# Batched matmul: four DRAM rows per partition, all transfers on one queue, casts and evacuations exchanged

## The chip, the core and the metric

The kernel runs on one core of one Trainium2 chip. The metric is the device time of one execution in microseconds; of the kernel before there are three runs, with a median of 133.25 us (132.75 to 133.29).

## The reference

For each of 16 batches the kernel computes the product of the transposed `a` with `b`. Both inputs are 512 x 512 float32, `a` is laid out as (k, m) and `b` as (k, n), and the output is float32 as well:

```python
batch, m, k, n = 16, 512, 512, 512
np.matmul(a.transpose(0, 2, 1), b).astype(np.float32)
```

`a` and `b` of one batch are 1 MB each, and so is the output: 33.55 MB are read and 16.78 MB are written in all.

## The kernel before

The unit of work is a batch. For each batch the kernel loads a whole matrix `a` and a whole matrix `b` into SBUF, casts both to bfloat16, multiplies them in 16 matmuls, and stores the whole output matrix. The contraction index k is split into KO = 4 groups of 128. The view `a_v` (line 24) is "bat (ko ki) m -> bat ki ko m": partition ki holds the DRAM rows ki, 128 + ki, 256 + ki and 384 + ki. A row is 512 float32, so each partition is filled from four separate pieces of 2 KB that lie 256 KB apart. `b_v` (line 25) is the same for `b`, and `out_v` (line 26) for the output, with the output row index m split into MO = 4 groups in the same way.

Every kind of buffer exists NB = 6 times. `load(bi)` (lines 50 to 53) issues the two 1 MB loads of a batch, one on the queue of SyncE (SP) and one on the queue of GpSimd (POOL), in turns: `a` of an even batch and `b` of an odd one go through SP. `cast(bi)` (lines 55 to 58) lets ScalarE (ACT) cast both matrices, 128 x 2048 elements at a time. `compute(bi)` (lines 60 to 73) makes, for each of the four groups mo of 128 output rows, an accumulation of four matmuls (line 65) into one of eight PSUM banks, and VectorE (DVE) copies the bank to the float32 output tile (line 72). The stationary operand of a matmul is a 128 x 128 block of contiguous columns of the cast `a`; the moving operand is 128 x 512 of the cast `b`. At the end ACT issues the store of the batch (line 73).

The order of the work is that of the Python loop, engine by engine: loads run five batches ahead of the matmuls and casts four batches ahead. ACT therefore has the casts of batch bi + 4 ahead of the store of batch bi in its queue. The transfers of the three queues (SP, POOL and ACT) share the core's 16 DMA engines. A DMA instruction waits on semaphores for the buffer it overwrites, and on that of an earlier DMA where a semaphore is used again.

Of the kernel before, what the change touches and what calls it, by code (L numbers as in the profile page):

```python
# [1 line left out]

# [4 lines left out]


@with_exitstack
def kernel(  # L10
    ctx: ExitStack,
    tc: tile.TileContext,
    a: bass.AP,
    b: bass.AP,
    out: bass.AP,
):
    nc = tc.nc
    P = 128
    batch, K, M = a.shape
    _, _, N = b.shape  # L20
    KO = K // P
    MO = M // P

    a_v = a.rearrange("bat (ko ki) m -> bat ki ko m", ki=P)
    b_v = b.rearrange("bat (ko ki) n -> bat ki ko n", ki=P)
    out_v = out.rearrange("bat (mo mi) n -> bat mi mo n", mi=P)

    f32 = mybir.dt.float32
    bf = mybir.dt.bfloat16
    NB = 6  # L30
    a_pool = ctx.enter_context(tc.tile_pool(name="a_pool", bufs=1))
    b_pool = ctx.enter_context(tc.tile_pool(name="b_pool", bufs=1))
    abf_pool = ctx.enter_context(tc.tile_pool(name="abf_pool", bufs=1))
    bbf_pool = ctx.enter_context(tc.tile_pool(name="bbf_pool", bufs=1))
    o_pool = ctx.enter_context(tc.tile_pool(name="o_pool", bufs=1))
    psum = ctx.enter_context(tc.tile_pool(name="ps", bufs=1, space=bass.MemoryType.PSUM))

    a_ts = [a_pool.tile([P, KO, M], f32, name=f"a{j}") for j in range(NB)]
    b_ts = [b_pool.tile([P, KO, N], f32, name=f"b{j}") for j in range(NB)]
    abf_ts = [abf_pool.tile([P, KO, M], bf, name=f"abf{j}") for j in range(NB)]  # L40
    bbf_ts = [bbf_pool.tile([P, KO, N], bf, name=f"bbf{j}") for j in range(NB)]
    o_ts = [o_pool.tile([P, MO, N], f32, name=f"o{j}") for j in range(NB)]
    psum_ts = [psum.tile([P, N], f32, name=f"ps{j}") for j in range(8)]

    in_eng = [nc.sync, nc.gpsimd]
    out_eng = nc.scalar

    engs = [nc.sync, nc.gpsimd]

    def load(bi):  # L50
        j = bi % NB
        engs[bi % 2].dma_start(a_ts[j][:], a_v[bi])  # L52
        engs[(bi + 1) % 2].dma_start(b_ts[j][:], b_v[bi])  # L53

    def cast(bi):
        j = bi % NB
        nc.scalar.copy(out=abf_ts[j][:], in_=a_ts[j][:])  # L57
        nc.scalar.copy(out=bbf_ts[j][:], in_=b_ts[j][:])  # L58

    def compute(bi):  # L60
        j = bi % NB
        for mo in range(MO):
            pt = psum_ts[(bi * MO + mo) % 8]
            for ko in range(KO):
                nc.tensor.matmul(  # L65
                    pt[:],
                    abf_ts[j][:, ko, mo * P:(mo + 1) * P],
                    bbf_ts[j][:, ko, :],
                    start=(ko == 0),
                    stop=(ko == KO - 1),  # L70
                )
            nc.vector.tensor_copy(out=o_ts[j][:, mo, :], in_=pt[:])  # L72
        nc.scalar.dma_start(out_v[bi], o_ts[j][:])  # L73

    for bi in range(min(NB - 1, batch)):
        load(bi)
    for bi in range(min(NB - 2, batch)):
        cast(bi)
    for bi in range(batch):
        if bi + NB - 1 < batch:  # L80
            load(bi + NB - 1)
        if bi + NB - 2 < batch:
            cast(bi + NB - 2)
        compute(bi)


# [1 line left out]
_INS = ['a', 'b']  # L88
_OUTS = [((16, 512, 512), 'float32')]


# [23 lines left out]
```

## Time and profile before

| What | Value |
|---|---|
| Median of three runs | 133.25 us |
| Profiled execution, span from first to last instruction | 131.4 us |
| Median of the runs less that span | 1.85 us |
| Busy share of the span: PE, DVE, ACT, POOL | 51%, 33%, 46%, 9% |
| DMA in the span | 50.38 MB, mean 383 GB/s |
| The chain that ended last, share on DMA | 73% |
| Mean of one matmul, one weight load, one PSUM copy, one cast | 429, 108, 691, 1896 ns |

The profiled execution's own time is known by its span alone; the 1.85 us between it and the median of the runs are taken as what lies around the span. A busy share tells how long an engine had work, and the 40 slices tell when. The share of a DMA queue in a window is the sum of its packets' durations over 16 engines times the window, so a packet's mean duration can be worked out from the share and the packet count. The shares of all queues can add up to a little over 100%, since a packet begins before the one ahead of it on the engine has ended.

### The profile page before, as it was taken

The numbers are of one execution on the slowest core, as the hardware profiler recorded it, in microseconds if no ns is written. First come the engines' busy times: TensorE is split into PE (matmuls) and PEld (weight loads), VectorE is DVE, ScalarE is ACT, GpSimd is POOL, SyncE is SP. The second block draws the span as 40 slices with busy tenths as digits, with TensorE's granted clock in tenths as the row PEclk, the third lists the DMA queues.
The fourth block names the chain that finished last, engine by engine and source line by source line (L and its number), as shares of the span: only waits on it lengthen the run. The fifth ranks groups of instructions, "written<-read, shape, count | busy, mean of one in ns | idle before, by whom it ended". The sixth has DMA issues, their size and how long they took to land.

```text
span 131.4 us, 806 instructions
## 1 busy us (share of the span) xinstructions
PE 67.5 (51%) x251; PEld 27.6 (21%) x256; DVE 43.9 (33%) x64; ACT 60.4 (46%) x33; POOL 12.3 (9%) x20
## 2 busy tenths in 40 slices
PE   0000899656406975004994049912992894991000
PEld 0000334223102331001341014401340341440000
DVE  0000248462501356000466006720474446672000
ACT  3054396923088140069310696049809949900000
POOL 6700220220003100002200022000000000000000
PEclk9999999999995599955589658997799999999555
DMA  2999999999999999999999999999999999999991
GB/s 88 362 390 390 383 393 386 390 385 384 387 390 402 414 411 406 413 416 406 410 409 416 410 408 413 413 384 393 409 358 403 409 406 403 409 409 409 409 397 64
DMA packets 21252, 50.38 MB, mean 383 GB/s; under 512 B 768, under 2 KB 768, under 8 KB 21248
## 3 DMA queue, kind: packets, MB, share of 16 engines
q1 hardware_dynamic: 8448, 16.78, 34.2%
q10 hardware_dynamic: 8448, 16.78, 33.0%
q0 software_dynamic: 4352, 16.78, 32.6%
q8 instruction: 2, 0.03, 0.1%
q14 instruction: 2, 0.02, 0.0%
HBM read 33.55 MB, written 16.78 MB: 383 GB/s over the span
## 4 chain that ended last, share of the span: by engine, by line
DMA 73%; SPq 7%; PE 5%; ACT 3%; issue 1%; DVE 1%; ACTq 0%
DMA b<-in_b_dram 54%; DMA a<-in_a_dram 19%; PE ps L65 5%; SPq L52 5%; ACT bbf L58 3%; SPq L53 2%; DVE o L72 1%; ACTq L73 0%; ACTq L57 0%; ACT abf L57 0%; ACTq L58 0%
## 5 line engine op out<-in xcount | busy, mean ns | idle before, releaser
L65 PE MATMUL ps<-bbf,abf 128*128 128x512 bf16 x251 | 67.5, 429 | 51.1 <-ACT bbf L58 50.7
L72 DVE COPY o<-ps 128x512 f32<-128x512 f32 x64 | 43.9, 691 | 75.5 <-PE ps L65 60.9
L57 ACT CAST abf<-a 128x2048 bf16<-128x2048 f32 x16 | 30.3, 1896 | 41.7 <-DMA a<-in_a_dram 37.8
L65 PEld LDWEIGHTS <-abf 128*128 128x128 bf16 x256 | 27.6, 108 | 90.5 <-issue 35.8
L58 ACT CAST bbf<-b 128x2048 bf16<-128x2048 f32 x16 | 30.3, 1895 | 12.2 <-DMA b<-in_b_dram 12.1
L53 POOL DMA_DIRECT2D b<-in_b_dram x8 | 6.1, 766 | 60.0 <-ACT bbf L58 59.2
L52 POOL DMA_DIRECT2D a<-in_a_dram x8 | 6.0, 749 | 7.6 <-ACT abf L57 7.6
L57 ACT ACT_TABLE_LOAD x1 | 1.3, 1283 | 0.7 <-PEq L99 0.7
L99 POOL MEMSET const-float32-0.0<- 128x1 f32 x1 | 0.1, 98 | 0.2 <-issue 0.2
L99 POOL MEMSET const-bfloat16-1.0<- 128x1 bf16 x1 | 0.1, 101 | 0.0
L99 POOL MEMSET const-uint8-127<- 128x1 uint8 x1 | 0.1, 99 | 0.0
L99 POOL MEMSET const-float32-1.0<- 128x1 f32 x1 | 0.1, 98 | 0.0
## 6 DMA issues: line engine op xcount, KB each, us to landing
out_dram<-o ACTq DMA_DIRECT2D x16, 1024.0 KB, 11.6
a<-in_a_dram SPq DMA_DIRECT2D x8, 1024.0 KB, 30.3
b<-in_b_dram SPq DMA_DIRECT2D x8, 1024.0 KB, 28.9
b<-in_b_dram POOLq DMA_DIRECT2D x8, 1024.0 KB, 16.5
a<-in_a_dram POOLq DMA_DIRECT2D x8, 1024.0 KB, 19.9
```

Source lines behind the costliest of these rows:

```text
L52: engs[bi % 2].dma_start(a_ts[j][:], a_v[bi])
L53: engs[(bi + 1) % 2].dma_start(b_ts[j][:], b_v[bi])
L57: nc.scalar.copy(out=abf_ts[j][:], in_=a_ts[j][:])
L58: nc.scalar.copy(out=bbf_ts[j][:], in_=b_ts[j][:])
L65: nc.tensor.matmul(pt[:], abf_ts[j][:, ko, mo * P:(mo + 1) * P], bbf_ts[j][:, ko, :], start=(ko == 0), stop=(ko == KO - 1),)
L72: nc.vector.tensor_copy(out=o_ts[j][:, mo, :], in_=pt[:])
L99: nc = _bacc.Bacc("TRN2", target_bir_lowering=False, num_devices=1)
```

## The change

The three DRAM views are written the other way round: `a_v`, `b_v` and `out_v` now give partition p the four consecutive DRAM rows 4p to 4p + 3. For `a` and `b` this is another split of k, the same for both, so that the sum is the same. For the output, group mo now consists of the rows m = 4 mi + mo. The stationary operand has to hold these columns, so it is taken from the cast `a` with a step of four elements (8 bytes) instead of a contiguous block.

All DMAs are issued by SP: loads of `a` and `b`, and stores. Loads run LAG = 4 batches ahead, and the store of batch i is put behind the loads of batch i + 4. There are now five buffers for loads, three for the cast matrices and six for outputs. The casts move from ACT to DVE and stand directly ahead of the matmuls of their own batch; the copies from PSUM move from DVE to ACT. The matmuls, their number and order within a batch are the same.

```diff
-    a_v = a.rearrange("bat (ko ki) m -> bat ki ko m", ki=P)
-    b_v = b.rearrange("bat (ko ki) n -> bat ki ko n", ki=P)
-    out_v = out.rearrange("bat (mo mi) n -> bat mi mo n", mi=P)
-    NB = 6
+    a_v = a.rearrange("bat (ki ko) m -> bat ki ko m", ko=KO)
+    b_v = b.rearrange("bat (ki ko) n -> bat ki ko n", ko=KO)
+    out_v = out.rearrange("bat (mi mo) n -> bat mi mo n", mo=MO)
+    LAG = 4
+    NL = LAG + 1
+    NB = 3
+    NO = LAG + 2
...
-    def load(bi):
-        j = bi % NB
-        engs[bi % 2].dma_start(a_ts[j][:], a_v[bi])
-        engs[(bi + 1) % 2].dma_start(b_ts[j][:], b_v[bi])
+    def load(i):
+        nc.sync.dma_start(a_ts[i % NL][:], a_v[i])
+        nc.sync.dma_start(b_ts[i % NL][:], b_v[i])
+    def store(i):
+        nc.sync.dma_start(out_v[i], o_ts[i % NO][:])
-    def cast(bi):
-        j = bi % NB
-        nc.scalar.copy(out=abf_ts[j][:], in_=a_ts[j][:])
-        nc.scalar.copy(out=bbf_ts[j][:], in_=b_ts[j][:])
...
+        nc.vector.tensor_copy(out=af[:], in_=a_ts[i % NL][:])
+        nc.vector.tensor_copy(out=bff[:], in_=b_ts[i % NL][:])
+        a_m = af[:].rearrange("p ko (mi mo) -> p ko mo mi", mo=MO)
...
-                    abf_ts[j][:, ko, mo * P:(mo + 1) * P],
-                    bbf_ts[j][:, ko, :],
+                    a_m[:, ko, mo, :],
+                    bff[:, ko, :],
...
-            nc.vector.tensor_copy(out=o_ts[j][:, mo, :], in_=pt[:])
-        nc.scalar.dma_start(out_v[bi], o_ts[j][:])
+            nc.scalar.copy(out=o[:, mo, :], in_=pt[:])
-    for bi in range(min(NB - 1, batch)):
-        load(bi)
-    for bi in range(min(NB - 2, batch)):
-        cast(bi)
-    for bi in range(batch):
-        if bi + NB - 1 < batch:
-            load(bi + NB - 1)
-        if bi + NB - 2 < batch:
-            cast(bi + NB - 2)
-        compute(bi)
+    for i in range(min(LAG, batch)):
+        load(i)
+    for i in range(batch):
+        if i + LAG < batch:
+            load(i + LAG)
+        compute(i)
+        store(i)
```

How the DMA queue of SP changes is seen in its order. Before, it holds half of the loads; a number behind a name is a buffer's, and the semaphores that an instruction waits for stand in brackets (DMAHW ones are set by transfers that have landed, Activation and DVE by those engines). These are its first rows:

```order
L52 DMA a_73<-in_a_dram 128x4x512
L53 DMA b_80<-in_b_dram 128x4x512
L52 DMA a_75<-in_a_dram 128x4x512
L53 DMA b_82<-in_b_dram 128x4x512
L52 DMA a_77<-in_a_dram 128x4x512
L53 DMA b_84<-in_b_dram 128x4x512
L52 DMA a_73<-in_a_dram 128x4x512 [waits DMAHW0_49,Activation_49]
L53 DMA b_80<-in_b_dram 128x4x512 [waits DMAHW1_49,Activation_49]
```

After the change, the same queue has every transfer. From the fourth batch's loads on it reads:

```order
L46 DMA a_64<-in_a_dram 128x2048
L47 DMA b_69<-in_b_dram 128x2048
L46 DMA a_65<-in_a_dram 128x2048 [waits DMAHW0_49]
L47 DMA b_70<-in_b_dram 128x2048 [waits DMAHW1_49]
L50 DMA out_dram<-o_77 128x2048 [waits DMAHW2_49,Activation_49]
L46 DMA a_61<-in_a_dram 128x2048 [waits DMAHW3_49,DVE_49]
L47 DMA b_66<-in_b_dram 128x2048 [waits DMAHW4_49,DVE_49]
L50 DMA out_dram<-o_78 128x2048 [waits DMAHW5_49,Activation_49]
```

A transfer is now 128 rows of 2048 elements, where it was 128 x 4 rows of 512. Eight semaphores go round, so that each DMA also waits until the eighth one ahead of it has landed, and the loads behind a store can't be issued before ACT has finished that store's tile. At the end of the queue five stores follow one another:

```order
L46 DMA a_61<-in_a_dram 128x2048 [waits DMAHW1_49,DVE_49]
L47 DMA b_66<-in_b_dram 128x2048 [waits DMAHW2_49,DVE_49]
L50 DMA out_dram<-o_82 128x2048 [waits DMAHW3_49,Activation_49]
L50 DMA out_dram<-o_77 128x2048 [waits DMAHW4_49,Activation_49]
L50 DMA out_dram<-o_78 128x2048 [waits DMAHW5_49,Activation_49]
L50 DMA out_dram<-o_79 128x2048 [waits DMAHW6_49,Activation_49]
L50 DMA out_dram<-o_80 128x2048 [waits DMAHW7_49,Activation_49]
```

The two load rows are those of batch 15, and the stores behind them are those of batches 11 to 15.

More of the change, by code (lines that the diff above doesn't have):

```diff
@@ L22 @@
     MO = M // P
-    a_v = a.rearrange("bat (ko ki) m -> bat ki ko m", ki=P)
-    b_v = b.rearrange("bat (ko ki) n -> bat ki ko n", ki=P)
-    out_v = out.rearrange("bat (mo mi) n -> bat mi mo n", mi=P)
     f32 = mybir.dt.float32
     bf = mybir.dt.bfloat16
-    NB = 6
[L31 to L34, printed above, removed]
@@ L35 @@
-    o_pool = ctx.enter_context(tc.tile_pool(name="o_pool", bufs=1))
-    psum = ctx.enter_context(tc.tile_pool(name="ps", bufs=1, space=bass.MemoryType.PSUM))
[L38 to L48, printed above, removed]
-    def load(bi):
-        j = bi % NB
-        engs[bi % 2].dma_start(a_ts[j][:], a_v[bi])
-        engs[(bi + 1) % 2].dma_start(b_ts[j][:], b_v[bi])
-    def cast(bi):
-        j = bi % NB
[L57 to L61, printed above, removed]
+    a_v = a.rearrange("bat (ki ko) m -> bat ki ko m", ko=KO)
@@ new lines @@
+    b_v = b.rearrange("bat (ki ko) n -> bat ki ko n", ko=KO)
[4 more added lines that the diff above has]
+    NO = LAG + 2
+    pool = ctx.enter_context(tc.tile_pool(name="sb", bufs=1))
+    psum = ctx.enter_context(tc.tile_pool(name="ps", bufs=1, space=bass.MemoryType.PSUM))
+    a_ts = [pool.tile([P, KO, M], f32, name=f"a{j}") for j in range(NL)]
+    b_ts = [pool.tile([P, KO, N], f32, name=f"b{j}") for j in range(NL)]
+    abf_ts = [pool.tile([P, KO, M], bf, name=f"abf{j}") for j in range(NB)]
@@ new lines, with compute @@
+    bbf_ts = [pool.tile([P, KO, N], bf, name=f"bbf{j}") for j in range(NB)]
+    o_ts = [pool.tile([P, MO, N], f32, name=f"o{j}") for j in range(NO)]
+    ps_ts = [psum.tile([P, N], f32, name=f"ps{j}") for j in range(8)]
+    def load(i):
[3 more added lines that the diff above has]
+        nc.sync.dma_start(out_v[i], o_ts[i % NO][:])
+    def compute(i):
+        af, bff = abf_ts[i % NB], bbf_ts[i % NB]
+        o = o_ts[i % NO]
+        nc.vector.tensor_copy(out=af[:], in_=a_ts[i % NL][:])
+        nc.vector.tensor_copy(out=bff[:], in_=b_ts[i % NL][:])
+        a_m = af[:].rearrange("p ko (mi mo) -> p ko mo mi", mo=MO)
@@ L62, in compute @@
         for mo in range(MO):
-            pt = psum_ts[(bi * MO + mo) % 8]
+            pt = ps_ts[(i * MO + mo) % 8]
             for ko in range(KO):
```

## Prediction

> **What bounds the kernel now.** I read the page's chain of waits first, then its slices, and then cut the span into windows. On the page:
>
> ```profile
> span 131.4 us, 806 instructions
> PE 67.5 (51%) x251; PEld 27.6 (21%) x256; DVE 43.9 (33%) x64; ACT 60.4 (46%) x33; POOL 12.3 (9%) x20
> DMA  2999999999999999999999999999999999999991
> DMA 73%; SPq 7%; PE 5%; ACT 3%; issue 1%; DVE 1%; ACTq 0%
> DMA packets 21252, 50.38 MB, mean 383 GB/s; under 512 B 768, under 2 KB 768, under 8 KB 21248
> ```
>
> No engine is busy for much more than half of the span, the chain that ended last lies to 73% on transfers, and the DMA engines are full from the second slice to the last but one. So the time is bytes divided by a rate, plus what is lost at both ends. The rate isn't the same everywhere. The windows (from, to, length, then each engine's work, granted clock, DMA share and GB/s) show it:
>
> ```profile
> 20.00:36.00 16.00, 10.38 (x46) 4.37 (x45) 8.78 (x13) 7.40 (x4) 1.50 (x2) 1.00 1.03 387
> 48.00:60.00 12.00, 3.07 (x15) 1.28 (x13) 2.77 (x4) 3.05 (x2) 0.00 (x0) 0.84 1.04 412
> 112.00:120.00 8.00, 6.58 (x30) 2.73 (x28) 5.53 (x8) 2.97 (x2) 0.00 (x0) 1.00 1.05 409
> 120.00:128.00 8.00, 0.00 (x0) 0.00 (x0) 0.00 (x0) 0.00 (x0) 0.00 (x0) 0.57 1.04 406
> 128.00:131.40 3.40, 0.00 (x0) 0.00 (x0) 0.00 (x0) 0.00 (x0) 0.00 (x0) 0.50 0.19 73
> ```
>
> The queues of three windows tell what moved in them: 20 to 36 us (only the two load queues), 48 to 60 us (loads and stores), and 120 to 128 us (only stores, 406 GB/s):
>
> ```profile
> q0 software_dynamic: 1060, 4.08, 66.5%
> q1 hardware_dynamic: 1064, 2.11, 36.9%
> ...
> q0 software_dynamic: 624, 2.39, 48.8%
> q10 hardware_dynamic: 637, 1.27, 27.4%
> q1 hardware_dynamic: 633, 1.26, 27.2%
> ...
> q10 hardware_dynamic: 1638, 3.25, 104.4%
> ```
>
> Loads alone go at 387 GB/s, stores alone at 406 to 409, and both together at 412. The DMA share is above 1 each time: the engines are full at all three rates. The last data are late by little, but two stretches are nearly empty. The window 0 to 6 us holds
>
> ```profile
> DMA packets 626, 1.25 MB, mean 208 GB/s; under 512 B 16, under 2 KB 16, under 8 KB 626
> ```
>
> At 400 GB/s, 1.25 MB take 3.1 us, so the start loses 2.9 us. The last window moves 73 x 3.4 = 0.25 MB, which is 0.6 us of work at 406, so the end loses 2.8. Together they are 5.7 us; what is left, 131.4 - 5.7 = 125.7 us for 50.38 MB, is 401 GB/s, which fits between the windows. **The check of the sum** is therefore 125.7 + 5.7 = 131.4 us of span, and 1.85 us more to the median of the runs (133.25).
>
> **Part 1: four rows in one piece.** What does a packet cost as it grows? From 48 to 60 us, the SP queue's 1.26 MB are 615 packets of 2 KB (the other 18 are the small semaphore writes): 27.2% of 16 x 12 us are 52.2 us, or 84.9 ns each. The POOL queue's 2.39 MB are 583 packets of 4 KB: 48.8% are 93.7 us, or 160 ns each. Twice the bytes cost 75.1 ns more, so 9.8 ns are a packet's own. One of 8 KB would then take 160 + 2 x 75.1 = 310 ns. There is a single row for that size, from 106 to 107 us, where one of 206 packets isn't under 8 KB:
>
> ```profile
> DMA packets 206, 0.41 MB, mean 410 GB/s; under 512 B 9, under 2 KB 9, under 8 KB 205
> q14 instruction: 1, 0.01, 1.9%
> ```
>
> 1.9% of 16 us are 0.30 us, the same figure. Since the shares add up to 1.04, packets overlap by some 4.6 ns: 84.9 - 4.6 = 80.3 ns for 2 KB on 16 engines is the 408 GB/s seen. With 305.6 ns an 8 KB packet would go at 429 GB/s; that, rounded to 430, is the upper end for loads and stores. The lower end is no effect, 406 for stores and 387 for loads.
>
> *Stores.* The same model makes 416 of the window from 48 to 60 us, half of whose bytes are in 4 KB packets, and 412 were seen, about half of the gain over 408. I take a little over half of the way from 406 to 430: 422 GB/s, 16.78 / 0.422 = 39.8 us.
>
> *Loads.* Alone they are slower for a reason that no row names. In the window from 20 to 36 us, 4 KB cost 66.5% of 256 us over 996 packets, 171 ns, and 2 KB cost 36.9% over 1030, 91.7 ns. By the same steps an 8 KB packet costs 171 + 2 x 79.3 = 330 ns there, or 403 GB/s. If the slowness comes from the scattered pieces, it goes, and 430 is the end. I take 412, between 403 and 422, which is also the rate of the window in which three quarters of the bytes were loads: 33.55 / 0.412 = 81.4 us.
>
> The Trainium skill (HBM Reference, "Specifications (TRN2)") says that one core streaming alone measures about 425 GB/s. The sum with 425 for everything would be 126.5 us. No window of this profile reaches 425; the fastest long one has 412.
>
> **Part 2: one queue.** Sixteen stores leave ACT's queue and 16 loads POOL's, all behind one another on SP. Issue is no bound:
>
> ```profile
> 0.74 0.42 SPq L52 DMA_DIRECT2D a<-in_a_dram  x1
> 3.35 5.65 SPq L52 DMA_DIRECT2D a<-in_a_dram  x1
> ```
>
> The first costs 0.42 us (the second is held up with four ahead of it, while the DMA engines are full): 48 x 0.42 = 20 us spread over the span, where each has 2.5 us of data. The new wait is that of a store for ACT, with the loads of batch i + 5 queued behind it. That batch i is ready follows from the distance: between the landing of its loads and the issue of its store, which waits for the eighth DMA ahead of it, five more 1 MB transfers land, 5.24 / 0.415 = 12.6 us. Casts, matmuls and copies of a batch must take less:
>
> ```profile
> 24.51 3.61 PE L65 MATMUL ps<-bbf,abf 128*128 128x512 bf16 x16 [1.30 <-ACT bbf L58]
> 24.51 3.33 PEld L65 LDWEIGHTS <-abf 128*128 128x128 bf16 x16 [1.58 <-issue]
> L65 PE MATMUL ps<-bbf,abf 128*128 128x512 bf16 x251 | 67.5, 429 | 51.1 <-ACT bbf L58 50.7 <-issue 0.2
> L72 DVE COPY o<-ps 128x512 f32<-128x512 f32 x64 | 43.9, 691 | 75.5 <-PE ps L65 60.9 <-remote 10.8 <-DMA out_dram<-o 3.7
> L57 ACT CAST abf<-a 128x2048 bf16<-128x2048 f32 x16 | 30.3, 1896 | 41.7 <-DMA a<-in_a_dram 37.8 <-PE ps L65 4.0
> L65 PEld LDWEIGHTS <-abf 128*128 128x128 bf16 x256 | 27.6, 108 | 90.5 <-issue 35.8 <-ACT abf L57 33.0
> ```
>
> 16 matmuls take 3.6 us at full clock and 16 x 429 = 6.9 us at the mean. The last cast on DVE has no row: at most 4 x 691 = 2.8 us for four times the elements, at least half of ACT's 1.9, so 1.0. A copy on ACT has none either: at most 1.9 (a quarter of that work), at least 1.9 / 4 = 0.5; I take DVE's 0.7, its own shape. That makes 2.8 + 6.9 + 0.7 = 10.4 us at worst, under 12.6. While one store is waited for, up to seven transfers (17 us) are outstanding. Cost nothing; without that cover it would be some microseconds per batch.
>
> **Part 3: casts and copies exchanged.** Per batch, DVE gets 2 x 2.8 = 5.6 us at most and ACT 4 x 0.7 = 2.8, both below the 7.6 us that a batch's 3.15 MB take. Even at its upper end (4 x 1.9 = 7.6) ACT would just keep up. Nothing on the path.
>
> **Part 4: the strided weights.** No row has a weight load with steps. Below, the cost is nothing; above, PE becomes the bound once a pair of load and matmul takes over 7.6 / 16 = 475 ns. The 16 loads at 208 ns lie under 16 matmuls today, and loads four times the 108 ns (432) would still fit beside the matmuls. I take nothing. The Trainium skill (SBUF — State Buffer, "Door 1: The DMA port swizzle") has a rule against such steps: full rate wants at least two accesses per 16-byte line. A step of 8 bytes gives two, so by it the loads keep their rate; no run here shows it yet.
>
> **Part 5: the end.** Behind the last load there are four stores, 4.19 / 0.422 = 9.9 us, as cover for batch 15: last cast 1.0 to 2.8, matmuls 3.6 to 6.9, copy 0.7, issue 0.4, and about 1.1 from the issue to the first packet (issue at 0.74; first bytes after 1.8 us, in the slices of 0 to 3 us):
>
> ```profile
> GB/s 0 0 0 0 0 0 0 0 0 0 0 0 0 0 0 0 0 0 0 0 0 0 0 0 137 109 164 137 109 109 109 0 27 137 82 246 218 382 382 410
> ```
>
> This is 6.8 to 11.9 us, so a gap of 0 to 2.0 us. I take 0.5. The losses at both ends otherwise stay at 5.7.
>
> **Sum:** 81.4 + 39.8 + 5.7 + 0.5 = 127.4 us of span, and with 1.85 **129.3 us**, 3.0% faster. The ends of the unknown costs: all at 430 is 117.0 + 5.7 + 1.85 = 124.6; 387 and 406 with a gap of 2.0 is 86.7 + 41.3 + 5.7 + 2.0 + 1.85 = 137.6.
>
> The Trainium skill (DMA: Bandwidth & Descriptors, "iDMA fabric") gives 408.7 GB/s for a load stream from SP with 4 KB rows. By that the loads would take 82.1 us and the sum 130.0. The 387 seen here for pieces of 2 KB lies below it.
>
> **Rivals.**
> (a) *Reading is the bound once nothing is mixed with it.* With one ring, an engine moves 2 MB of loads, then 1 MB of stores, and the mixture that had 412 is gone. If reading alone stays at 387 whatever the piece, the sum is 86.7 + 39.8 + 5.7 + 0.5 + 1.85 = 134.5 us, 1% slower. For it speaks that 4 KB packets are slowed in the load window too (171 against 160 ns); against it, that the transfers of one ring can overlap at the seams, and that 330 ns for 8 KB would already be 403. It decides below 390 GB/s for loads (133.9 us).
> (b) *The full price of packets holds for reads too*: 117.0 + 5.7 + 0.5 + 1.85 = 125.1 us. For it: the 0.30 us packet. Against it: the gain in the mixed window was half of the model's.
> (c) *The change doesn't do what it says, or helps little*: rows of 8 KB are cut into 4 KB packets again, or loads reach only 390 to 396 GB/s. With 396 for loads and 412 for stores: 84.7 + 40.7 + 0.5 + 5.7 + 1.85 = 133.5 us, no change.
> (d) *PE becomes the bound*: if a strided weight load doesn't hide and the clock stays low, a pair costs 429 + 108 = 537 ns, and 256 of them 137.5 us; with some 10 us until the first matmul, about 150. It decides from 475 ns a pair. Against it: PE has 49% of the span free.
>
> **How the numbers follow.** Forecast (loads 396 to 422 GB/s) 0.58, (a) 0.12, (b) 0.14, (c) 0.12, (d) 0.04. A measurement of this kernel can tell about 0.5% from no change (132.6 to 133.9 us). Faster is the forecast and (b), 0.72; same is (c), 0.12; slower is (a) and (d), 0.16. The range reaches from (b) to (a), 125.0 to 134.6 us; (d), and the far ends of (a) and (b), about 0.15 in all, lie outside. The likeliest case's own range is 127 to 132.
>
> **What would show it.** The packet counts: some 2,048 of 8 KB per 16.78 MB, and each near 305 to 310 ns. Slices with only loads (the first four batches) at 400 GB/s and more carry part 1; at 387 they speak for (a). Idle DMA slices in the middle, with SP waiting for ACT, would break part 2; a weight load far above 208 ns with PE on the chain, part 4; a dip in the last slices shows part 5. The prediction is wrong if loads stay under 396 GB/s with large packets, or if DMA isn't full any more.

## The result and the profile after

The changed kernel takes 126.59 us (median of four runs, 125.6 to 126.76); the kernel before takes 133.03 us beside it. The ratio is 0.950, with a 95% interval from 0.945 to 0.955. The forecast was 129.3 us, so the direction is right, and the gain is 6.4 us where 4 were expected. Ratios, here and below, leave out executions that took over 1.5% longer than the fastest of their kernel.

The page of the changed kernel, in the same lines as were shown of the one before, and with the one queue that it has left:

```profile
span 125.0 us, 807 instructions
PE 73.1 (59%) x256; PEld 30.4 (24%) x256; DVE 39.3 (31%) x32; ACT 38.8 (31%) x65; POOL 0.2 (0%) x4
...
DMA  2999999999999999999999999999999999999980
GB/s 89 414 430 430 430 425 420 420 341 425 425 422 417 412 427 427 425 435 422 427 425 425 433 425 427 425 425 435 425 425 425 420 422 435 422 425 425 422 365 34
DMA packets 6916, 50.38 MB, mean 403 GB/s; under 512 B 768, under 2 KB 768, under 8 KB 768
q1 hardware_dynamic: 6912, 50.33, 96.3%
...
DMA 83%; PE 7%; DVE 2%; ACT 1%; issue 0%; SPq 0%; DVEq 0%; ACTq 0%
```

It is the same kind of picture: DMA is full from the second slice on, and transfers are 83% of the chain that ended last. But there are 6,912 packets where there were 21,248. Apart from the 768 small semaphore writes all are 8 KB. The queue's share gives 0.963 x 16 x 125.0 = 1926 us for all packets; less some 7 us for the small ones (9 ns each in the trace), that is 312 ns for one of the 6,144 large ones. The level in the slices is mostly 412 to 435 GB/s, with one slice of 341. By stage (the same columns as the windows before; from 6 to 24 us there are only loads, from 112 us on only stores):

```profile
6.00:12.00 6.00, 2.56 (x7) 1.01 (x8) 3.39 (x3) 0.59 (x1) 0.00 (x0) 1.00 1.02 430
18.00:24.00 6.00, 3.68 (x17) 1.73 (x16) 3.32 (x3) 2.93 (x5) 0.00 (x0) 1.00 1.02 426
24.00:36.00 12.00, 7.29 (x32) 3.46 (x32) 4.04 (x4) 4.69 (x8) 0.00 (x0) 1.00 1.00 401
48.00:60.00 12.00, 7.48 (x29) 3.16 (x27) 3.71 (x4) 4.69 (x8) 0.00 (x0) 0.91 1.01 427
112.00:116.00 4.00, 3.09 (x16) 1.52 (x14) 1.11 (x1) 1.76 (x3) 0.00 (x0) 1.00 1.01 428
120.00:125.00 5.00, 0.00 (x0) 0.00 (x0) 0.00 (x0) 0.00 (x0) 0.00 (x0) 0.68 0.33 138
```

Loads alone went from 387 to 426 GB/s (423 to 430 in windows of 6 us), stores alone from 406 to 428, and the mixture from 412 to 427. All three stages are now at nearly one rate. Two places are not: the window from 24 to 36 us, and the end.

### The profile page after: what moved, and what is told of

Its sections match the earlier page's. It is cut to its first block, busy times and chain, and to the rows that moved or that the text cites. A ratio compares the mean times of both kernels' runs of the same rounds, so it can differ in the third digit from the quotient of the medians.

```text
span 125.0 us, 807 instructions
## 1 busy us (share of the span) xinstructions
PE 73.1 (59%) x256; PEld 30.4 (24%) x256; DVE 39.3 (31%) x32; ACT 38.8 (31%) x65; POOL 0.2 (0%) x4
## 3 DMA queue, kind: packets, MB, share of 16 engines
q1 hardware_dynamic: 6912, 50.33, 96.3%
HBM read 33.55 MB, written 16.78 MB: 403 GB/s over the span
## 4 chain that ended last, share of the span: by engine, by line
DMA 83%; PE 7%; DVE 2%; ACT 1%; issue 0%; SPq 0%; DVEq 0%; ACTq 0%
DMA b<-in_b_dram 38%; DMA out_dram<-o 29%; DMA a<-in_a_dram 16%; PE ps L61 7%; DVE bbf L56 2%; ACT o L68 1%; SPq L46 0%; SPq L47 0%; DVEq L56 0%; ACTq L68 0%; SPq L50 0%
## 5 line engine op out<-in xcount | busy, mean ns | idle before, releaser
L61 PE MATMUL ps<-bbf,abf 128*128 128x512 bf16 x256 | 73.1, 451 | 43.7 <-DVE bbf L56 43.7
L68 ACT COPY o<-ps 128x512 f32<-128x512 f32 x64 | 37.5, 586 | 78.0 <-PE ps L61 78.0
L61 PEld LDWEIGHTS <-abf 128*128 128x128 bf16 x256 | 30.4, 124 | 85.9 <-DVE bbf L56 40.9
L55 DVE CAST abf<-a 128x2048 bf16<-128x2048 f32 x16 | 19.6, 1227 | 52.2 <-DMA a<-in_a_dram 26.1
L56 DVE CAST bbf<-b 128x2048 bf16<-128x2048 f32 x16 | 19.6, 1227 | 21.6 <-DMA b<-in_b_dram 21.6
```

Of the source, the lines that this page charges most:

```text
L55: nc.vector.tensor_copy(out=af[:], in_=a_ts[i % NL][:])
L56: nc.vector.tensor_copy(out=bff[:], in_=b_ts[i % NL][:])
L61: nc.tensor.matmul(pt[:], a_m[:, ko, mo, :], bff[:, ko, :], start=(ko == 0), stop=(ko == KO - 1),)
L68: nc.scalar.copy(out=o[:, mo, :], in_=pt[:])
```

## The experiments

All kernels ran beside the kernel before on the same chip, and ratios are to that. Two theories stand against each other at first. P: a packet has a price of its own, so that the larger piece is the gain. Q: several queues, and GpSimd's above all, held the rates down, so that the one SP queue is the gain.

### The old pieces on the new queue

```diff
-    a_v = a.rearrange("bat (ki ko) m -> bat ki ko m", ko=KO)
+    a_v = a.rearrange("bat (ko ki) m -> bat ki ko m", ki=P)
...
-        a_m = af[:].rearrange("p ko (mi mo) -> p ko mo mi", mo=MO)
+        a_m = af[:].rearrange("p ko (mo mi) -> p ko mo mi", mi=P)
```

(`b_v` and `out_v` alike.)

> The changed kernel with the old DRAM views again: a partition gets four pieces of 2 KB that lie 256 KB apart, and the stationary operand is contiguous; one SP queue, order and engines stay as changed. Theory P (a packet has a price of its own, so the gain is the 8 KB piece): the rates of the kernel before come back, stores near 408 GB/s and loads 387 to 408, so 131 to 135.3 us, no faster than before. Theory Q (the load queue of GpSimd and the mixture of three queues held the rates down, one SP queue is the gain): everything stays near 427 GB/s and the time is 126 to 128 us.

It took 134.23 us, a ratio of 1.012 (1.008 to 1.016): about 1% slower than before the change, and as theory P expected. Its windows:

```profile
18.00:24.00 6.00, 4.72 (x23) 1.98 (x22) 2.61 (x3) 3.16 (x6) 0.00 (x0) 1.00 1.05 387
60.00:72.00 12.00, 6.53 (x18) 2.13 (x16) 4.75 (x4) 3.01 (x6) 0.00 (x0) 0.72 1.05 406
```

Loads alone are back at exactly 387 GB/s, with SP's queue alone. So it was neither GpSimd's queue nor the number of queues that held them there, and Q falls. The mixture has 406 and not the 412 of before. That fits the packets: the kernel before had half of its loads in GpSimd's packets of 4 KB, and this one has 2 KB throughout (25,344 packets in all).

### The new pieces on the old queues

```diff
-    a_v = a.rearrange("bat (ko ki) m -> bat ki ko m", ki=P)
+    a_v = a.rearrange("bat (ki ko) m -> bat ki ko m", ko=KO)
...
-                    abf_ts[j][:, ko, mo * P:(mo + 1) * P],
+                    a_m[:, ko, mo, :],
```

(`b_v` and `out_v` alike, and `a_m` as in the changed kernel; three queues, order, buffers and engines are those of before.)

> The kernel before with the new DRAM views alone (8 KB pieces and the strided stationary operand); its three queues, its order, its buffers and its engines stay. Theory P: all windows go to 420 to 430 GB/s, and the time is 126 to 127.5 us, like the changed kernel. Theory Q: loads through two queues stay near 390 to 400 GB/s while no store runs, and the time is 129 to 132 us.

It took 125.23 us, 0.945 (0.941 to 0.948), a little less than either theory expected. Until its first store is issued at 30.8 us there are only loads, through SP and GpSimd; the second window is the mixture:

```profile
18.00:24.00 6.00, 5.07 (x24) 2.49 (x23) 4.02 (x6) 5.18 (x3) 1.05 (x2) 1.00 1.03 427
60.00:72.00 12.00, 6.91 (x27) 3.10 (x26) 4.84 (x7) 6.36 (x4) 1.05 (x2) 0.78 1.01 428
```

The views alone bring the whole gain, and a little more than the whole change does. What else was changed gives nothing and costs about 1%, with the old pieces (134.23 us, ratio 1.012) as with the new ones; the last experiments look at this difference.

### Size of the piece, and its place in DRAM

The old views differ from the new in two things: the piece is smaller, and the pieces of a partition lie 256 KB apart. To tell the two apart, 16 unused elements are put behind each row of the load tiles in SBUF: they cut the loads into pieces while the DRAM rows stay consecutive.

```diff
-    a_ts = [pool.tile([P, KO, M], f32, name=f"a{j}") for j in range(NL)]
+    a_ts = [pool.tile([P, KO, M + 16], f32, name=f"a{j}") for j in range(NL)]
...
-        nc.sync.dma_start(a_ts[i % NL][:], a_v[i])
+        nc.sync.dma_start(a_ts[i % NL][:, :, 0:M], a_v[i])
```

(`b` alike; the casts read the same part of the tiles.)

> The changed kernel, but each row of the load tiles in SBUF is followed by 16 unused elements, so that a load is cut into pieces of 2 KB again while it still reads four consecutive DRAM rows per partition; stores keep 8 KB. It tells the size of the piece from its place in DRAM. If the size alone set the 387 GB/s of loads, they stay at 387 to 395 while alone: 33.55 / 0.39 + 16.78 / 0.427 + 5.9 + 1.6 = 132.8 us. If the scattered rows held loads down, they now reach the 408 GB/s of 2 KB packets: 82.2 + 39.3 + 5.9 + 1.6 = 129.0 us.

It took 130.37 us, 0.984 (0.979 to 0.988). The second kernel pads every other row, for pieces of 4 KB:

```diff
-    a_ts = [pool.tile([P, KO, M], f32, name=f"a{j}") for j in range(NL)]
+    a_ts = [pool.tile([P, 2, 2 * M + 16], f32, name=f"a{j}") for j in range(NL)]
```

(`b` alike; loads and casts take two rows of DRAM as one row of the tile.)

> As the kernel with 2 KB load pieces, but 16 unused elements follow every second row, so that loads are cut into pieces of 4 KB of consecutive DRAM; stores keep 8 KB. A price per packet, fitted to loads alone at 398 GB/s with 2 KB (82.3 ns a packet on each of 16 engines) and 427 with 8 KB (307 ns), is 7.4 ns plus 74.9 ns for each 2 KB, so 4 KB takes 157 ns, 417 GB/s, and the time is 80.5 + 39.3 + 5.9 + 1.6 = 127.3 us, up to 1.5 more if the last store comes late. If instead only a cut into the old 2 KB pieces hurts, 4 KB runs at 427 and the time is 126.6 us.

It took 127.89 us, 0.962 (0.960 to 0.965). Windows with only loads, of the 2 KB pieces first, then of the 4 KB ones:

```profile
12.00:18.00 6.00, 5.93 (x25) 2.81 (x24) 3.08 (x3) 3.48 (x6) 0.00 (x0) 1.00 1.05 398
```

```profile
12.00:24.00 12.00, 10.25 (x44) 4.75 (x42) 5.39 (x6) 6.53 (x12) 0.00 (x0) 1.00 1.03 415
```

For loads alone this gives a row of four: 387 GB/s for 2 KB scattered, 398 for 2 KB consecutive, 415 for 4 KB, and 426 for 8 KB. Of the 39 between the first and the last, 11 go with the place and 28 with the size. (The padding in SBUF is also new between the first and the second; it wasn't tried by itself.) Worked out from these rates, on 16 engines, the last three are 82.3, 157.9 and 307.7 ns a packet: 75.6 ns for 2 KB more, and 149.8 for 4 KB more, which is a straight line with about 7 ns of its own for each packet. The 2 KB kernel lies between its two expectations, 1.4 us over the lower: its loads alone have 398 and not 408 GB/s, and its last store comes late (87 GB/s from 123.2 to 124.8 us); what each is worth wasn't measured. The 4 KB kernel is 0.6 us over its own.

### Loads and stores on different queues

```diff
-        nc.sync.dma_start(out_v[i], o_ts[i % NO][:])
+        nc.scalar.dma_start(out_v[i], o_ts[i % NO][:])
```

> The changed kernel with its stores issued by ACT instead of SP, so that loads don't stand behind stores and the DMA engines have loads and stores of two queues at a time. If the order of loads and stores within one ring matters (one direction at a time is faster, or slower, than a mixture), the rate of the middle moves away from 427 GB/s, for example to the 412 of the mixed window before: 50.33 / 0.412 + 5.9 + 1.6 = 129.7 us. If only the packet sets the rate, it stays at 425 to 428 and the time at 126 to 127 us.

Its four executions lie between 128.0 and 133.3 us, too far apart for a ratio, and none took the 126 to 127 us expected; the profile is of the shortest.

```profile
60.00:72.00 12.00, 9.91 (x32) 3.88 (x32) 4.92 (x5) 4.41 (x8) 0.00 (x0) 0.73 1.02 429
96.00:108.00 12.00, 8.22 (x23) 3.21 (x25) 3.69 (x4) 2.94 (x5) 0.00 (x0) 0.69 1.01 427
116.00:120.00 4.00, 2.83 (x13) 1.50 (x14) 1.14 (x1) 1.76 (x3) 0.00 (x0) 1.00 0.72 297
```

With loads and stores mixed, the middle has the same 427 to 429: loads and stores in one queue or in two make no difference to the rate at this size. The end does. A store is issued as soon as its batch is done, none is left behind the last load, and DMA waits for the last two batches: the window from 116 to 120 us has 297 GB/s, and from 120.2 to 122.2 us nothing moves. So the stores that are held back are a cover for the end, where the loads run ahead like this.

### The distance between loads and stores

```diff
-    LAG = 4
+    LAG = 1
```

> The changed kernel with loads only one batch ahead (LAG = 1: two load buffers of each kind, three output buffers); a store stands one batch of loads behind its own. If the wait of a store for ACT is covered by the distance alone, it now shows: the issue of a store and the loads behind it waits for the copies of its batch, and from there it takes 1.1 us to the first packet, 7.4 us for the 3 MB, some 1.5 us until they have landed, and 5.5 to 8.7 us of cast, matmuls and copy, for two batches: 7.8 to 9.4 us a batch in place of 7.4, so 133 to 157 us, with dips of the DMA rate in every batch. If the distance had nothing to do with it, it stays at 127 us.

The ratio is 1.157 (1.152 to 1.163), so about 154 us, near the upper end. All six executions lie between 153.4 and 157.8 us, and the slices are those of the longest:

```profile
GB/s 162 430 424 327 222 258 424 384 155 325 327 418 403 239 336 367 432 279 201 323 336 430 321 287 401 405 392 313 323 401 426 277 222 348 327 424 292 136 201 204
```

The rate still touches 430 in between, but falls every time that SP stands at a store and waits for ACT, with the next loads queued behind it. These waits (us in total, times, longest) are

```profile
SPq L50 <- ACT o L68: 120.4, 16, 14.9
```

With LAG = 2:

> The changed kernel with loads two batches ahead (LAG = 2). The same sum gives 15.5 to 18.7 us for three batches, 5.2 to 6.2 us each, less than the 7.4 us of their data, so the middle stays full at about 427 GB/s. Only two stores, 4.9 us, now lie behind the last load, against 7 to 10 us of work for the last batch, so the end has a gap of 2 to 5 us: 128.5 to 131.5 us. A rival by which the depth of the queue sets the rate would lower the rate of the middle too.

It took 130.15 us, 0.976 (0.971 to 0.982). The middle is full and the end is short of cover, both as expected:

```profile
48.00:60.00 12.00, 6.25 (x19) 2.47 (x21) 3.68 (x3) 2.34 (x4) 0.00 (x0) 0.72 1.01 427
84.00:96.00 12.00, 7.43 (x27) 2.99 (x25) 4.83 (x4) 4.10 (x7) 0.00 (x0) 0.87 1.01 427
116.00:120.00 4.00, 1.96 (x10) 0.95 (x10) 1.23 (x1) 1.18 (x3) 0.00 (x0) 1.00 0.70 289
```

```profile
SPq L50 <- ACT o L68: 96.9, 16, 10.9
```

SP waits 96.9 us for ACT here, and it costs nothing in the middle: the transfers that were issued earlier cover it. Only the end pays. And with five:

> The changed kernel with loads five batches ahead (LAG = 5, six load buffers of each kind, seven output buffers), so that five stores lie behind the last load. If the end of the changed kernel is short of cover in some executions, the fifth store (2.5 us) takes that away: 125.5 to 126.5 us, with less spread. If the end is set by DMA engines that finish late, nothing changes: 126.6 us.

It took 126.12 us, 0.949 (0.946 to 0.953), not to be told from LAG = 4, which had 0.953 (0.950 to 0.956) beside it. The spread isn't less either: 125.4 to 126.7 us against 126.3 to 127.0. Four is enough.

### Casts and copies on their old engines

```diff
-        nc.vector.tensor_copy(out=af[:], in_=a_ts[i % NL][:])
-        nc.vector.tensor_copy(out=bff[:], in_=b_ts[i % NL][:])
+        nc.scalar.copy(out=af[:], in_=a_ts[i % NL][:])
+        nc.scalar.copy(out=bff[:], in_=b_ts[i % NL][:])
...
-            nc.scalar.copy(out=o[:, mo, :], in_=pt[:])
+            nc.vector.tensor_copy(out=o[:, mo, :], in_=pt[:])
```

> The changed kernel with casts on ACT and copies from PSUM on DVE, as before the change; views, queue and order stay as changed. If the exchange of engines is hidden by the transfers, the middle stays at 427 GB/s, and only the end can feel that the last cast takes 1.9 in place of 1.23 us and the last copy 0.69 in place of 0.59: 126.6 to 127.6 us. If the exchange was part of the gain, it is 129 us or more.

It took 126.38 us, 0.951 (0.946 to 0.957). The exchange is hidden and gives nothing.

### The three-queue kernel against the changed one

The changed kernel once more, the kernel before with the new views once more, and a mixture of both, all on one chip:

> The changed kernel once more, beside the three others on one chip: 126.0 to 127 us.

> The kernel before with 8 KB pieces alone, once more: if its 125.2 us were really less than the changed kernel, it is again 1 to 1.5 us under it; if that was the chip, both agree within 0.5 us.

```diff
-        nc.sync.dma_start(b_ts[i % NL][:], b_v[i])
+        nc.gpsimd.dma_start(b_ts[i % NL][:], b_v[i])
```

(Casts and copies are on their old engines, as in the last section.)

> The changed kernel with the loads of b on GpSimd's queue and with casts on ACT and copies on DVE as before; stores stay four batches behind on SP. If two load queues are what makes the three-queue kernel end earlier, this is as fast, 125 to 125.5 us, or faster, since it keeps the cover of four stores; if only the packets count, it is 126 to 127 us.

The changed kernel took 126.50 us (126.29 to 127.04), the three-queue kernel 125.25 (125.16 to 125.36), and the mixture has a ratio of 0.951 (0.948 to 0.955), like the changed kernel. So a second load queue alone isn't what makes the three-queue kernel shorter. One of the mixture's seven executions, the profiled one, took 242.37 us, where the others took 126.0 to 127.2: a matmul took 1102 ns in it on average, against 451 in the changed kernel, at a granted clock of 1.00. What slowed it stays open, and its profile isn't used here. The three-queue kernel with 8 KB pieces is thus better than both kernels of the study, by 1.0% against the changed one and 5.7% against the one before. Where the 1.25 us lie is read from the same windows of both. The changed kernel:

```profile
24.00:30.00 6.00, 3.59 (x15) 1.72 (x16) 2.42 (x3) 2.35 (x4) 0.00 (x0) 1.00 0.98 341
30.00:36.00 6.00, 5.33 (x16) 2.04 (x16) 1.55 (x2) 2.01 (x4) 0.00 (x0) 0.72 1.02 406
108.00:112.00 4.00, 2.57 (x9) 0.91 (x7) 1.58 (x2) 1.76 (x3) 0.00 (x0) 0.84 1.00 422
116.00:120.00 4.00, 2.06 (x9) 0.84 (x8) 0.00 (x0) 1.76 (x3) 0.00 (x0) 0.99 0.96 403
```

and the three-queue kernel:

```profile
24.00:30.00 6.00, 3.29 (x14) 1.59 (x14) 2.77 (x4) 4.25 (x3) 0.53 (x1) 0.94 1.01 421
30.00:36.00 6.00, 5.78 (x23) 2.65 (x23) 3.22 (x5) 3.05 (x2) 0.53 (x1) 0.78 1.01 414
108.00:112.00 4.00, 1.33 (x8) 0.59 (x6) 1.68 (x3) 3.70 (x2) 0.00 (x0) 1.00 0.87 358
116.00:120.00 4.00, 0.00 (x0) 0.00 (x0) 0.31 (x1) 0.00 (x0) 0.00 (x0) 0.75 1.02 422
```

Against 426 GB/s, the changed kernel loses 6 x (1 - 341/426) + 6 x (1 - 406/426) = 1.5 us between 24 and 36 us, where the other loses 0.2. (In the first profile of the changed kernel the same stretch, at 401 GB/s, loses 0.7.) The other loses 0.6 us from 108 to 112, while its last stores wait for their batches, and the changed one nearly nothing there. The rest is the end. The loss after 24 us is at the place where the first store follows the five batches of loads in the queue. With LAG = 5 it comes later (first a window of the changed kernel, then one of LAG = 5):

```profile
26.00:28.00 2.00, 2.00 (x10) 0.87 (x8) 0.88 (x1) 1.28 (x3) 0.00 (x0) 1.00 0.92 311
```

```profile
26.00:28.00 2.00, 2.00 (x11) 0.92 (x9) 1.03 (x1) 1.43 (x3) 0.00 (x0) 1.00 1.00 418
31.00:33.00 2.00, 2.00 (x11) 0.91 (x8) 1.00 (x1) 1.41 (x3) 0.00 (x0) 1.00 0.99 311
```

A batch of loads more moves it by 5 us, which is the time of 2 MB. So it belongs to the first change from loads to stores and not to the time. It needs no shared queue: with the stores on ACT's queue, the first of which is issued at 16.5 us, the window from 18 to 24 us has 396 GB/s. And it is hardly seen with smaller load packets: from 24 to 36 us the kernel with scattered 2 KB pieces has 391 GB/s, and those with consecutive pieces of 2 and 4 KB have 404 and 416, each a little over its own rate for loads alone. The engines are busy nearly all the time while it lasts, but the packets take longer. From 24 to 30 us of the second profile of the changed kernel:

```profile
DMA packets 282, 2.05 MB, mean 341 GB/s; under 512 B 32, under 2 KB 32, under 8 KB 32
q1 hardware_dynamic: 282, 2.05, 98.5%
```

98.5% of 16 x 6 us are 94.6 us for 250 packets of 8 KB, 378 ns each in place of 312. Why, no run shows.

## Why the prediction was right, and what was mis-sized

The direction and the mechanism were right, but the case that was given 0.58 didn't come: it had loads at 396 to 422 GB/s and a time of 127 to 132 us, but loads alone have 426, and the time is 126.6. What came is rival (b), the full price of packets for loads as well, which had 0.14. The stated range holds the measured time because it reaches down to (b).

**What bounds the kernel** was right: bytes at a rate, and something lost at both ends. The sum with measured terms nearly closes: 33.55 / 0.426 = 78.8 us for loads, 16.78 / 0.427 = 39.3 for stores, 5.9 at the ends (the first 6 us hold 246 GB/s, 1.48 MB or 3.5 us of work; the last 5 hold 138 GB/s, 0.69 MB or 1.6 us), and 12 x (1 - 401/426) = 0.7 for the slow place, 124.7 us of the 125.0 measured.

**Part 1, the price of a packet,** was right in its mechanism, and its 310 ns stand beside 312 measured. The terms that were mis-sized are the two rates: the step that failed is what was made of it, "I take 412" for loads and "a little over half of the way" for stores. The full price held for both: 426 to 428 GB/s, next to the upper end of 430. The loads were 2.6 us too dear, the stores 0.5, the gap at the end 0.5 and what lies around the span 0.25 (1.6 us and not 1.85). The slow place (0.7 us, not foreseen), the ends (5.9 and not 5.7) and the 0.3 us by which the sum doesn't close give some of it back, and 2.7 us of error are left.

The first reason for the low rates was that the mixed window had shown half of the model's gain, 412 over a start of 408. (The model makes 415 of that window rather than 416.) The start was too high: 408 is what stores alone have (406 to 409), and 4.6 ns is the overlap by which 2 KB packets come out there. The kernel with the old pieces on the new queue mixes loads and stores in packets of 2 KB alone, and its windows from 36 to 108 us have 396 to 406. As far as it can stand for the kernel before, 412 is a gain of 6 at the least, where the model has 7. The second reason was the slowness of loads alone, which was extended to 8 KB as 403 GB/s. That was wrong: packets of 2 KB are slowed by their place, from 398 to 387, and this goes with the new view; the rest of the gap was the size. Rival (b) came nearest, 125.1 against 126.6 us. Of the 1.5 us between, 1.1 are rates of 426 and 427 in place of 430, and 0.7 the slow place; the smaller terms above make up the rest.

**The Trainium skill** (HBM Reference, "Specifications (TRN2)") had 425 GB/s for a core alone, and an estimate of 126.5 us came out of it. The windows of the changed kernel between 36 and 116 us, with 421 to 428, agree with that, where those of before had not reached it. The 408.7 that the Trainium skill gives for rows of 4 KB (DMA: Bandwidth & Descriptors, "iDMA fabric") are a little under the 415 that loads in 4 KB pieces show here.

**Rival (a), reading as the bound,** fell: loads alone on one queue have 430 and 426 GB/s, and mixing them with stores gives 427. **Rival (c)** fell with the packet count. **Rival (d)** fell too: a weight load has 124 ns on average, and 16 of them lie under 16 matmuls at full clock:

```profile
113.16 3.17 PEld L61 LDWEIGHTS <-abf 128*128 128x128 bf16 x16 [1.39 <-DVE bbf L56]
113.16 3.65 PE L61 MATMUL ps<-bbf,abf 128*128 128x512 bf16 x16 [0.91 <-DVE bbf L56]
```

The 3.65 us are nearly the 3.61 of before, so the step of four elements costs no time on the path. The weight load itself does pay for it. These are its shortest, median and longest durations in ns, in the kernel before, in the changed one, and in the one with the old pieces on the new queue, whose weights are contiguous again:

```profile
L65 PEld LDWEIGHTS <-abf x256: 95/98/152, 8.3 to 118.0; 128*128 128x128 bf16 x128
L61 PEld LDWEIGHTS <-abf x256: 111/114/152, 7.0 to 116.2; 128*128 128x128 bf16 x128
L61 PEld LDWEIGHTS <-abf x256: 95/98/152, 7.4 to 125.0; 128*128 128x128 bf16 x128
```

The median is 16 ns longer with the step, and the matmuls hide it. By the Trainium skill's rule of 16-byte lines (SBUF — State Buffer, "Door 1: The DMA port swizzle") the loads would have kept their rate; the measurement says otherwise.

**Part 2, the one queue,** was right in that its waits are covered, but it isn't always "the eighth DMA" that a store waits for. SP does wait for ACT:

```profile
SPq L50 <- ACT o L68: 23.3, 7, 10.1
```

Of these 23.3 us, 5.1 fall to the first two stores and 17.9 to the last five, behind which no loads are queued; between them it is under 1 us. They cost nothing, and LAG = 1 and 2 show where such waits begin to. **Part 3** was right: the cast takes 1227 ns on DVE (1.0 to 2.8 were the bounds) and the copy 586 ns on ACT (0.5 to 1.9), and putting both back changes nothing. **Part 5** was right in size: the gap before the last store, expected as 0.5 us, is nothing in the first profile of the changed kernel (424 GB/s from 116 to 120 us) and small in the second one (403).

## What to carry to other kernels

In a kernel whose DMA engines are always full, look at the size of the packets first. A straight line through two sizes of the mixed window gave the price of the third to 1%, and it would have served better than a damped guess. Some luck was in that: the same line through the window of loads alone gave 330 ns in place of 310, and no row told ahead of time which of the two would hold. Choose the split of a contraction index, and of the output rows, so that each partition gets one consecutive piece; it costs nothing on the path where the other operand can take the same split and the matmuls hide the weight loads, as here. Put the last stores so far behind their work that the last batch is covered, and expect nothing from fewer queues: here, one queue in place of three went with a time about 1% longer.

## What was not expected of the hardware

In the changed kernel the DMA engines don't seem to end together. The last windows of its transfers:

```profile
118.00:120.60 2.60, 0.00 (x0) 0.00 (x0) 0.00 (x0) 0.00 (x0) 0.00 (x0) 1.00 1.00 419
120.60:122.20 1.60, 0.00 (x0) 0.00 (x0) 0.00 (x0) 0.00 (x0) 0.00 (x0) 0.87 0.57 241
122.20:123.20 1.00, 0.00 (x0) 0.00 (x0) 0.00 (x0) 0.00 (x0) 0.00 (x0) 0.50 0.12 49
```

From 122.2 us on the DMA share is 0.12, the share of two of 16 engines, with 49 GB/s. It is some 2.5 us from where the rate falls to the last packets. The trace doesn't name a packet's engine, so which engines these are, whether all had the same bytes, and why some end late stays open. Five stores of cover in place of four don't change it (0.10 and 41 GB/s in the same window). The three-queue kernel, second profile, has no such tail:

```profile
120.60:122.20 1.60, 0.00 (x0) 0.00 (x0) 0.00 (x0) 0.00 (x0) 0.00 (x0) 0.50 0.67 277
122.20:123.40 1.20, 0.00 (x0) 0.00 (x0) 0.00 (x0) 0.00 (x0) 0.00 (x0) 0.50 0.00 0
```

Its last packet ends over 1 us earlier than that of the changed kernel, which is part of the 1.25 us between them. But the kernel before, with the same three queues, has a tail (a share of 0.14 from 129 to 130 us), so the number of queues alone doesn't decide it. The other surprises are the loss at the first store (two microseconds at 311 GB/s), and that GpSimd's queue in the kernel before had put two pieces of 2 KB into one packet of 4 KB (4,352 packets where SP's queue had 8,448 for the same bytes), which is why its windows could give the price of a larger packet at all.
